# Forgetting attention in a hybrid decoder block: when the weights of the last heads and of the gated unit are fetched

## The chip, the cores and the metric

The kernel runs on one core of a Trainium2 chip. The metric is the device time of one execution in microseconds (us). A core has five engines that each work through their own instructions in order and wait for each other by semaphores: TensorE (PE, matrix products), VectorE (DVE), ScalarE (ACT), GpSimd (POOL) and SyncE (SP). SP does no arithmetic here: it issues most of the DMA transfers, in order, and an issue that has to wait holds up those behind it.

## The reference

Batch 1, sequence 1024, width 1024, all float32. Cut to what matters:

```python
u = rms_norm(h, norm_mix)
u_ssm, q, k, v, f_logit, gate_logits = split(u @ w_in)
y_ssm = gelu(s5_ssm(u_ssm, ...))
glu_a, glu_b = split(y_ssm @ w_glu); out_a = glu_a * sigmoid(glu_b)
att = forgetting_attention(q, k, v, f_logit + b_forget)   # 8 heads of 64, causal softmax, bias from cumsum(log f)
h = h + (gate_a * out_a + gate_b * (att @ w_fox_o)) @ w_mix_out
h = h + memory_cross_attention(...)
h = h + (silu(f_a) * f_b) @ w_ffn_out
return rms_norm(h, norm_final)
```

## The kernel before

A float32 product is made of three products in a reduced format: each operand is split into a high part (`split`, L178: a cast on ACT) and a low part (L179: a subtraction, mostly on DVE), and `mm3` (L168 to L170) adds hi*hi, lo*hi and hi*lo in PSUM. So every weight is loaded into a tile `raw` (a ring of 4), cast on ACT to `whi`, subtracted on DVE to `wlo`, and then used by PE. ACT and DVE work in order, so a cast that waits for its transfer holds up everything behind it there.

The stages are: the input norm and the state-space branch (its output y lies in DRAM as `y_d`), the attention over 8 heads (`Fox.run`, about 300 to 592 us), the tail (gated unit, mixing, cross-attention, feed-forward). The attention is what the change touches. Its loop over heads `h` runs 12 units (two blocks of queries, 4 and 8 blocks of keys); `scores` makes a unit's scores on PE (L1655, L1656, bank `sc`), adds the causal mask on DVE (`trk`, L1658) on the diagonal, takes the exponential on ACT (`pf`, L1662), and splits it into `ph` (ACT L1667, or DVE L1664) and `pl` (DVE L1668 or POOL L1665); `values_hi` and `values_lo` multiply these with v (L1680, L1681, L1687). Between the units stand lists `side[0..11]` of other work for later heads:

- `pro[h + 2].parts` and `.evac`: q and k of the head after the next, 16 products of three matmuls (`uh`, `ul` are the halves of u; names `_0` and `_1` are its two halves of tokens), copied out to the tiles `hb` by L1597 to L1603;
- `row_max(h + 1)` (L1628 on PE, L1630 and L1633 on DVE) and `max_row` (L1642, L1644): the row maxima of the next head, which go by a small DMA (L1645, `hb<-mr`) into the operand of the next head's scores: those scores can't start before it has landed;
- `pro[h + 3].load` (L1575, L1576, two transfers of 256 KB in 256-byte pieces, called in `side[5]`) and `.split` in `side[9]`: the weights of the head three ahead;
- `finish(h - 1)` (L1698 to L1702: `rc<-num`, `rd_d<-rc`, `rb<-rd_d`) and `divide(h - 1)` (L1708, L178, L179, then L1714): the softmax denominator goes through DRAM to be spread over 64 partitions, and the head's result is divided by it;
- in head 6, `load_y` (L1733): y from `y_d` into tiles `yh`, `yl` that take the place of tiles of u, 16 transfers of 256 KB in 512-byte pieces; `gate_rows` (L1610, L1611) for the two gate rows of a later head;
- in head 7, the first products of the gated unit (`Glu.values(0..3)`): `load(j)` (two transfers of `wg_d`, 256 KB each, issued at L153) and `split`, then the products with y.

The order in the text is not the order on the engines: a scheduler moves instructions ahead where their operands allow it. `issue_after(ins)`, here called through `B.behind(ins)`, adds an edge from `ins` to each instruction of the block that is on the engine of `ins`: those are queued behind it there, without a semaphore. All transfers named in this change are issued by SP, so such a block binds only SP's transfers in it, not the casts on ACT or DVE.

Of the kernel before, what the change touches and what calls it, by code (L numbers as in the profile page):

```python
# [19 lines left out]
P = 128  # L20
D = 1024
L = 1024
NT = 8
GRP = 32
NH = 8
# [270 lines left out]
def hybrid_block_kernel(ctx: ExitStack, tc: tile.TileContext, x, mem, norm_mix, w_in, b_forget,  # L296
# [32 lines left out]
    with tc.tile_pool(name="fox", bufs=1, reuse_waits="tile") as fp:  # L329
        Fox(B, fp, sh, uT, w_in, b_forget[0], cum_d, rd_d, att_d).run(y_d, yT, aT, w_glu, wg_d,  # L330
                                                                       [f for j in range(4) for f in glu.values(j)])
    with tc.tile_pool(name="st2", bufs=1, reuse_waits="tile") as s2:
# [170 lines left out]
def stage_tail(B, big, s2, sh, x, glu, aT, gate_d, kv_d, w_fox_o, w_mix_out, g_mq, w_mem_q, w_mem_o, g_ffn,  # L503
# [19 lines left out]
    fox = {}  # L523

    def fox_part(j):
        if j % 2 == 0:
            fox[j // 2] = B.wblock(w_fox_o, 0, 4, j * P, 2 * P)
        fh, fl = fox[j // 2]
        o = (j % 2) * P
        sg = glu.out.pop(j)  # L530
        for h in range(2):
            cs = slice(512 * h, 512 * h + 512)
            po = B.bank("pv")
            B.gemm_t(po, fh[:, :, o:o + P], fl[:, :, o:o + P], aT, h, 4)
            gb = load(gate_d[D + j * P:D + (j + 1) * P, cs], "gb")
            V.tensor_mul(gb, gb, po)
            V.tensor_add(sg[:, cs], sg[:, cs], gb)
            mh, ml = mT.rhs(j, h)
            B.split(mh, ml, sg[:, cs])

    for j in range(8):
        if j > 3:
            for f in glu.values(j):
                f()
        glu.rest(j)
        if j > 2:
            fox_part(j - 3)
# [906 lines left out]
class Fox:  # L1454
# [90 lines left out]
    def setup(self):  # L1545
# [15 lines left out]
        self.pj, self.mc, self.pvs, self.num, self.rb, self.raw = {}, {}, {}, {}, {}, {}  # L1561
        self.hi_todo, self.lo_todo = [], []

# [73 lines left out]
    def max_row(self, h):  # L1637
        B = self.B
        mc = self.mc.pop(h)
        B.V.tensor_tensor(out=mc[:, 0, :], in0=mc[:, 0, :], in1=mc[:, 1, :], op=ALU.max)  # L1640
        pm = B.bank("misc")
        B.T.transpose(pm[0:NT, 0:P], mc[:, 0, :], B.ident)  # L1642
        mr = B.small.tile([NT, P], F32R, tag="mr", bufs=1, name="mr")
        B.V.tensor_scalar(out=mr, in0=pm[0:NT, 0:P], scalar1=-1.0, scalar2=None, op0=ALU.mult)  # L1644
        B.S.dma_start(f32(self.hb[h % 2][2][68:69, :]).rearrange("o (a b) -> o a b", a=NT), f32(mr))  # L1645

# [46 lines left out]
    def finish(self, h):  # L1693
# [7 lines left out]
        rb = self.fp.tile([64, L], F32, tag="rb", bufs=2, name="rb")  # L1701
        self.spread = S.dma_start(rb, self.rd_d[h].partition_broadcast(64))  # L1702
        self.rb[h] = rb
# [17 lines left out]
    def run(self, y_d, yT, aT, w_glu, w_d, filler):  # L1721
# [8 lines left out]
        def load_y(k, h):  # L1730

            for i, dst in enumerate(yT.rhs(k, h)):
                S.dma_start(f32(dst).rearrange("p (t c) -> p t c", t=4),  # L1733
                            y_d[k, i, 4 * h:4 * h + 4].rearrange("t p c -> p t c"))

# [33 lines left out]
        for h in range(NH):  # L1769
# [17 lines left out]
            if h + 3 < NH:  # L1787
                side[9].append(lambda: pro[h + 3].split(self.exp))
            if h > 0 and h + 3 < NH:
                side[5].append(lambda: pro[h + 3].load(self.spread))  # L1790
            if h == 0:
                side[0].append(lambda: self.values_of_v(0, 7))
            if late:
                for k in range(8):
                    side[4 + k].append(lambda k=k: load_y(k // 2, k % 2))
            if h == NH - 1:
                for k in range(3):
                    side[6 + k].append(lambda k=k: load_att(k))
                for i, f in enumerate(filler):
                    side[i * 12 // len(filler)].append(f)  # L1800
            for i, u in enumerate(units):
# [44 lines left out]
```

## Time and profile before

| what | us |
|---|---|
| median of 3 runs (1578.55 to 1581.72) | 1579.52 |
| the profiled execution's own time | 1578.99 |
| its span, first to last instruction | 1577.3 |
| PE busy in the span | 1529.5 |
| DVE busy | 1023.0 |
| ACT busy | 657.7 |

The page of the profile gives busy times per engine, groups of instructions by line with the idle time ahead of them and what ended it, and the chain that ended last. The timeline lists instructions with start, duration, engine, line, output and input, and in brackets the idle time ahead and its releaser. In the view by stretches each row has the stretch, its length, and for PE, PEld (the weight loads), DVE, ACT and POOL the busy time and the number of instructions, then the clock that was granted to TensorE (1.00 is full), the share of time in which the DMA engines were busy, and GB/s.

### The profile page before, as it was taken

The page shows a single profiled execution, that of the slowest core. Times are in us where ns is not written, and L with a number is a line of the kernel's source. Part 1 is how long each engine was busy: PE and PEld are TensorE (multiplying, and loading weights), DVE is VectorE, ACT ScalarE, POOL GpSimd, SP SyncE. Part 2 cuts the span into 40 slices and gives each one's busy share as a digit, 9 for nine tenths or more (in the row PEclk, how much of TensorE's full clock was granted, in tenths as well). Part 3 has the DMA queues.
Part 4 walks back from the last instruction along what each step waited for, and adds up shares of the span by engine and source line. Part 5 has one row for each costly group of instructions (what it writes and reads, how often), then busy time and mean ns, then how long its engine had stood idle before and what let it go on. Part 6 is the DMA issues. An engine that isn't in the chain of part 4 may idle for free.

```text
span 1577.3 us, 20371 instructions
## 1 busy us (share of the span) xinstructions
PE 1529.5 (97%) x7313; PEld 1258.4 (80%) x7313; DVE 1023.0 (65%) x1822; ACT 657.7 (42%) x1177; POOL 264.9 (17%) x343
## 2 busy tenths in 40 slices
PE   7799999999999899999999999999999999999997
PEld 6688888898777578878888788888888888788886
DVE  6756545444788677676455688777777775566555
ACT  6422434323566553232335565333333332354342
POOL 3026653200212124110001200100000000001001
PEclk8999999999999999999999999999999999999999
DMA  8753466332123746368411156554445543896642
GB/s 295 151 106 97 130 116 143 97 119 30 25 45 56 206 121 194 114 206 284 144 28 40 62 206 192 169 164 158 159 155 162 161 148 130 279 391 223 192 155 107
DMA packets 196101, 235.09 MB, mean 149 GB/s; under 512 B 35144, under 2 KB 127208, under 8 KB 195488
## 3 DMA queue, kind: packets, MB, share of 16 engines
q1 hardware_dynamic: 188512, 215.97, 46.6%
q10 hardware_dynamic: 7488, 17.83, 3.0%
q8 instruction: 57, 0.93, 0.2%
q14 instruction: 44, 0.36, 0.1%
HBM read 162.98 MB, written 72.71 MB: 149 GB/s over the span
## 4 chain that ended last, share of the span: by engine, by line
PE 80%; DVE 7%; DMA 5%; ACT 3%; POOL 2%; issue 2%; SPq 0%; POOLq 0%; ACTq 0%; DVEq 0%
PE mm L875 14%; PE mm L168 8%; PE mm L169 8%; PE mm L170 8%; PE pv L875 7%; PE mm L1015 4%; PE sc L875 4%; PE sc L168 3%; PE sc L170 3%; PE sc L169 3%; PE sc L1015 3%; PE pv L1015 3%; PE misc L1015 1%; DMA raw<-in_w_in_dram 1%; DMA raw<-in_w_mem_kv_dram 1%
## 5 line engine op out<-in xcount | busy, mean ns | idle before, releaser
L178 ACT CAST whi<-raw 128x1024 fp32r<-128x1024 f32 (+2 forms) x123 | 114.7, 940 | 176.7 <-PE mm L875 52.8
L179 DVE TENSOR_TENSOR wlo<-raw,whi 128x1024 fp32r<-128x1024 f32 (+2 forms) x120 | 127.7, 1069 | 73.2 <-ACT whi L178 71.3
L168 PE MATMUL mm<-uh,whi 128*128 128x512 f32 x344 | 137.5, 400 | 2.5 <-ACT whi L178 2.4
L179 DVE TENSOR_TENSOR ol<-or,oh 128x1024 fp32r<-128x1024 f32 x73 | 92.1, 1266 | 68.5 <-ACT oh L178 67.5
L170 PE MATMUL mm<-uh,wlo 128*128 128x512 f32 x344 | 135.2, 393 | 0.5 <-DVE wlo L179 0.5
L169 PE MATMUL mm<-ul,whi 128*128 128x512 f32 x344 | 135.4, 394 | 0.0
L178 ACT CAST oh<-or 128x1024 fp32r<-128x1024 f32 x73 | 76.9, 1053 | 104.5 <-PE mm L1015 35.2
L907 POOL TENSOR_TENSOR g<-a,c 128x512 f32<-128x512 f32 x22 | 35.8, 1627 | 386.8 <-ACT a L906 299.0
L1665 POOL TENSOR_TENSOR pl<-pf,ph 128x512 fp32r<-128x512 f32 (+1 forms) x32 | 37.8, 1181 | 242.7 <-DVE ph L1664 173.1
L168 PEld LDWEIGHTS mm<-uh,whi 128*128 128x128 f32 x344 | 65.2, 190 | 14.8 <-ACT whi L178 2.8
L170 PEld LDWEIGHTS mm<-uh,wlo 128*128 128x128 f32 x344 | 64.9, 189 | 14.7 <-DVE wlo L179 1.5
L169 PEld LDWEIGHTS mm<-ul,whi 128*128 128x128 f32 x344 | 65.2, 190 | 11.0
L197 POOL TENSOR_TENSOR r<-ms,mhalf 128x1 f32<-128x1 f32 (+1 forms) x30 | 19.4, 647 | 308.1 <-DVE ms L193 280.8
L1662 ACT ACTIVATE pf<-sc 128x512 f32<-128x512 f32 (+1 forms) x96 | 46.3, 489 | 45.0 <-DVE sc L1658 29.4
L875 PE MATMUL pv<-S3h,we 128*128 128x512 f32 x176 | 57.7, 389 | 0.0
L1131 POOL TENSOR_TENSOR sg<-sg,ga 128x512 f32<-128x512 f32 x16 | 30.5, 1928 | 72.7 <-DVE sg L1124 72.7
L1668 DVE TENSOR_TENSOR pl<-pf,ph 128x512 fp32r<-128x512 f32 (+2 forms) x64 | 35.8, 560 | 10.5 <-ACT ph L1667 9.7
L1015 PE MATMUL mm<-oh 128*128 128x512 f32 x106 | 41.2, 389 | 0.0
L1015 PE MATMUL mm<-ol,oh 128*128 128x512 f32 x106 | 41.2, 389 | 0.0
L1015 PE MATMUL mm<-oh,ol 128*128 128x512 f32 x106 | 41.2, 389 | 0.0
L178 ACT CAST we<-rawb 128x512 fp32r<-128x512 f32 x20 | 12.5, 624 | 68.9 <-PE pv L875 33.8
L168 PE MATMUL sc<-uh,whi 128*128 128x512 f32 x104 | 40.8, 393 | 0.0
(583 smaller groups left out, 4585.0 us busy)
## 6 DMA issues: line engine op xcount, KB each, us to landing
or<-c_d SPq DMA_DIRECT2D x77, 256.0 KB
raw<-in_w_in_dram SPq DMA_DIRECT2D x22, 512.0 KB
wo<-in_w_ffn_out_dram SPq DMA_DIRECT2D x22, 512.0 KB
c_d<-g SPq DMA_DIRECT2D x44, 256.0 KB
t_d<-wo SPq DMA_DIRECT2D x44, 256.0 KB
or<-t_d SPq DMA_DIRECT2D x44, 256.0 KB
rawb<-in_w_ffn_in_dram SPq DMA_DIRECT2D x20, 512.0 KB
raw<-in_w_ffn_in_dram SPq DMA_DIRECT2D x20, 512.0 KB
```

The costliest lines, as they stand in the source:

```text
L168: T.matmul(ps, lh, rh, start=first, stop=False)
L169: T.matmul(ps, lh, rl, start=False, stop=False)
L170: T.matmul(ps, ll, rh, start=False, stop=last)
L178: self.A.copy(hi, src)
L179: (self.G if pool_lo else self.V).tensor_sub(lo, src, f32(hi))
L875: T.matmul(ps, l_[:, k, :], r_, start=first and k == 0 and i == 0, stop=k == 3 and i == 2, skip_group_check=True)
L907: G.tensor_mul(g[:, 512:], a1, c1)
L1015: T.matmul(ps, l_[:, gi], r_[:, 512:], start=n < 3 and p == 0 and k == 0 or n == 7 and p == 0 and k == 0, stop=p == NP - 1 and k == 2, ski ...
L1131: self.B.G.tensor_mul(self.out[j][:, cs], self.out[j][:, cs], ga)
L1662: self.exp = A.activation(pf[:, off:], ps[:, off:], AF.Exp)
L1665: G.tensor_sub(pl[:, off:], pf[:, off:], f32(ph[:, off:]))
L1668: V.tensor_sub(pl[:, off:], pf[:, off:], f32(ph[:, off:]))
```

## The change

Four edits, all of them on the place of transfers in SP's queue:

1. The weights of heads 5, 6 and 7 are loaded one head sooner: heads 4 and 5 in head 1, head 6 in head 2, head 7 in head 3, each behind the spread of the denominators (`rb<-rd_d`) of the head before the one they are called in. The splits stay where they were.
2. `load_y` takes all first halves of the tokens before the second halves; the first halves are queued behind the spread of head 4, the second behind the maxima of head 6 (`hb<-mr`).
3. The loads of the gated unit in head 7's list are queued behind the spread of head 3 (the first three) or behind the maxima of head 6 (the fourth).
4. In the tail, loads of the later gated-unit weights and of `w_fox_o` are queued behind the maxima of head 6.

```diff
-        self.hi_todo, self.lo_todo = [], []
+        self.hi_todo, self.lo_todo, self.spread, self.maxima = [], [], {}, {}
...
-        B.S.dma_start(f32(self.hb[h % 2][2][68:69, :]).rearrange("o (a b) -> o a b", a=NT), f32(mr))
+        self.maxima[h] = B.S.dma_start(f32(self.hb[h % 2][2][68:69, :]).rearrange("o (a b) -> o a b", a=NT), f32(mr))
...
-        self.spread = S.dma_start(rb, self.rd_d[h].partition_broadcast(64))
+        self.spread[h] = S.dma_start(rb, self.rd_d[h].partition_broadcast(64))
...
-            for i, dst in enumerate(yT.rhs(k, h)):
-                S.dma_start(f32(dst).rearrange("p (t c) -> p t c", t=4),
-                            y_d[k, i, 4 * h:4 * h + 4].rearrange("t p c -> p t c"))
+            with B.behind(self.maxima[NH - 2] if h else self.spread[NH - 4]):
+                for i, dst in enumerate(yT.rhs(k, h)):
+                    S.dma_start(f32(dst).rearrange("p (t c) -> p t c", t=4),
+                                y_d[k, i, 4 * h:4 * h + 4].rearrange("t p c -> p t c"))
+
+        def first_glu(i, f):
+            with B.behind(self.spread[3] if i < 9 else self.maxima[NH - 2]):
+                f()
...
-            if h > 0 and h + 3 < NH:
-                side[5].append(lambda: pro[h + 3].load(self.spread))
+            for n_ in {1: (4, 5), 2: (6,), 3: (7,)}.get(h, ()):
+                side[5].append(lambda n_=n_: pro[n_].load(self.spread[h - 1]))
...
-                    side[4 + k].append(lambda k=k: load_y(k // 2, k % 2))
+                    side[4 + k].append(lambda k=k: load_y(k % 4, k // 4))
...
-                    side[i * 12 // len(filler)].append(f)
+                    side[i * 12 // len(filler)].append(lambda i=i, f=f: first_glu(i, f))
...
+    glu.after = fox.maxima[NH - 2]
...
-            fox[j // 2] = B.wblock(w_fox_o, 0, 4, j * P, 2 * P)
+            with B.behind(glu.after):
+                fox[j // 2] = B.wblock(w_fox_o, 0, 4, j * P, 2 * P)
...
-            for f in glu.values(j):
-                f()
+            with B.behind(glu.after):
+                for f in glu.values(j):
+                    f()
```

SP's queue in head 4, before: `raw_4939` is the weights of head 7, `raw_5601`, `raw_5685` and `raw_5770` are the first three of the gated unit, `att_d` is the result of head 3.

```order
L1698 DMA rc_4864<-num_4573 128x1x8
L1700 DMA rd_d_82<-rc_4864 128x8
L1702 DMA rb_4868<-rd_d_82 64x1024
L1575 DMA raw_4939<-in_w_in_dram 128x8x64
L1576 DMA raw_4939<-in_w_in_dram 128x8x64
L153 DMA raw_5601<-wg_d_2919 128x4x128 x2
L1714 DMA att_d_80<-ahi_4914 64x1024
L1714 DMA att_d_80<-alo_4915 64x1024
L153 DMA raw_5685<-wg_d_2919 128x4x128 x2
L153 DMA raw_5770<-wg_d_2919 128x4x128 x2
L1610 DMA hb_3220<-cum_d_81 2x1024
L1645 DMA hb2_3226<-mr_5021 1x8x128
```

The same place in the changed kernel (lines 3 higher).

```order
L1701 DMA rc_4867<-num_4576 128x1x8
L1703 DMA rd_d_82<-rc_4867 128x8
L1705 DMA rb_4871<-rd_d_82 64x1024
L153 DMA raw_5601<-wg_d_2919 128x4x128 x2
L153 DMA raw_5685<-wg_d_2919 128x4x128 x2
L153 DMA raw_5770<-wg_d_2919 128x4x128 x2
L1717 DMA att_d_80<-ahi_4917 64x1024
L1717 DMA att_d_80<-alo_4918 64x1024
L1613 DMA hb_3220<-cum_d_81 2x1024
L1648 DMA hb2_3226<-mr_5021 1x8x128
```

The weights of head 7 have left this place (they stand at the same place of head 3's queue now), and the gated unit's six transfers stand together ahead of head 3's result. On ACT the four casts that belong to these loads stand in the same places as before. In head 1's queue the two transfers of head 5 have been added: the first behind head 4's two, the second behind the result of head 0 and ahead of the gate rows of head 3 and the maxima of head 2.

SP's queue in head 5, before, behind the maxima of head 5: `rc`, `rd_d`, `rb` are head 4's denominators, `yh`, `yl` are y (the number in the middle is the half of the tokens).

```order
L1645 DMA hb2_3226<-mr_5021 1x8x128
L1611 DMA hb_3222<-cum_d_81 2x1024
L1733 DMA yh0_0_2900<-y_d_78 128x4x128
L1698 DMA rc_5146<-num_4858 128x1x8
L1733 DMA yl0_0_2904<-y_d_78 128x4x128
L1733 DMA yh0_1_2901<-y_d_78 128x4x128
L1733 DMA yl0_1_2905<-y_d_78 128x4x128
L1733 DMA yh0_0_2900<-y_d_78 128x4x128
L1733 DMA yl0_0_2904<-y_d_78 128x4x128
L1700 DMA rd_d_82<-rc_5146 128x8
```

The same place in the changed kernel.

```order
L1648 DMA hb2_3226<-mr_5021 1x8x128
L1614 DMA hb_3222<-cum_d_81 2x1024
L1701 DMA rc_5146<-num_4861 128x1x8
L1703 DMA rd_d_82<-rc_5146 128x8
L1705 DMA rb_5150<-rd_d_82 64x1024
L1737 DMA yh0_0_2900<-y_d_78 128x4x128
L1737 DMA yl0_0_2904<-y_d_78 128x4x128
L1737 DMA yh0_0_2900<-y_d_78 128x4x128
L1737 DMA yl0_0_2904<-y_d_78 128x4x128
L1737 DMA yh1_0_2902<-y_d_78 128x4x128
```

No transfer of y is left between the three steps of head 4's denominators; eight of the sixteen follow them, and the other eight come behind the maxima of head 6, seven of them ahead of the gate rows of head 7 and all eight ahead of the gated unit's fourth load.

ACT's order at the start of head 6, before: `whi_5857` is the cast of the gated unit's fourth weights.

```order
L1662 ACTIVATE pf_5334<-sc_5328 128x512
L1689 COPY num_5140<-pv_5232 65x512
L1667 CAST ph_5332<-pf_5334 128x512
L1662 ACTIVATE pf_5359<-sc_5353 128x384
L178 CAST whi_5857<-raw_5854 128x1024
L1667 CAST ph_5357<-pf_5359 128x384
L1662 ACTIVATE pf_5381<-sc_5375 128x256
L1597 ACTIVATE hb2_3226<-mm_5338 64x512
```

The same place in the changed kernel.

```order
L1665 ACTIVATE pf_5334<-sc_5328 128x512
L1670 CAST ph_5332<-pf_5334 128x512
L1665 ACTIVATE pf_5359<-sc_5353 128x384
L1670 CAST ph_5357<-pf_5359 128x384
L1665 ACTIVATE pf_5381<-sc_5375 128x256
L1692 COPY num_5140<-pv_5232 65x512
L1665 ACTIVATE pf_5412<-sc_5406 128x128
L1670 CAST ph_5410<-pf_5412 128x128
```

The cast no longer stands between an exponential and its `ph`; it comes 12 places later, behind `pf_5488`, a unit of the second block of queries. Its subtraction on DVE moves to the end of head 6.

More of the change, by code (lines that the diff above doesn't have):

```diff
@@ L329, in hybrid_block_kernel @@
     with tc.tile_pool(name="fox", bufs=1, reuse_waits="tile") as fp:
-        Fox(B, fp, sh, uT, w_in, b_forget[0], cum_d, rd_d, att_d).run(y_d, yT, aT, w_glu, wg_d,
-                                                                       [f for j in range(4) for f in glu.values(j)])
+        fox = Fox(B, fp, sh, uT, w_in, b_forget[0], cum_d, rd_d, att_d)
+        fox.run(y_d, yT, aT, w_glu, wg_d, [f for j in range(4) for f in glu.values(j)])
+    glu.after = fox.maxima[NH - 2]
     with tc.tile_pool(name="st2", bufs=1, reuse_waits="tile") as s2:
```

## Prediction

> **What bounds the kernel now.** I read the page first, then PE's waits, then the attention in stretches, then the timelines of the engines that PE's longest waits lead to.
>
> ```profile
> PE 1529.5 (97%) x7313; PEld 1258.4 (80%) x7313; DVE 1023.0 (65%) x1822; ACT 657.7 (42%) x1177; POOL 264.9 (17%) x343
> PE 80%; DVE 7%; DMA 5%; ACT 3%; POOL 2%; issue 2%; SPq 0%; POOLq 0%; ACTq 0%; DVEq 0%
> ```
>
> PE is busy for 97% of the span and carries 80% of the chain that ended last. So a change of transfers alone is worth only what PE waits for them, directly or through ACT and DVE. PE's waits from 500 to 580 us (total, times, longest) name the releasers:
>
> ```profile
> PE mm L168 <- ACT whi L178: 2.4, 1, 2.4
> PE pv L1680 <- ACT ph L1667: 2.2, 3, 1.0
> PE sc L1655 <- ACT pf L1662: 2.1, 2, 1.7
> PE mm L170 <- DVE wlo L179: 0.5, 1, 0.5
> PE mm L1628 <- ACT hb L1603: 0.5, 1, 0.5
> ```
>
> Heads 5 and 6 lie here, with 7.7 us of waits. In stretches (busy time of PE, PEld, DVE, ACT, POOL, then granted clock, DMA share, GB/s):
>
> ```profile
> 488.60:512.80 24.20, 24.17 (x119) 18.44 (x118) 19.59 (x51) 15.10 (x30) 4.60 (x4) 1.00 0.27 39
> 512.80:519.70 6.90, 3.39 (x15) 1.78 (x14) 1.88 (x5) 2.78 (x4) 0.00 (x0) 1.00 0.96 266
> 519.70:526.50 6.80, 5.84 (x18) 4.24 (x19) 5.37 (x7) 5.02 (x9) 0.00 (x0) 0.50 0.24 70
> 526.50:539.70 13.20, 13.20 (x67) 10.05 (x65) 10.06 (x30) 7.63 (x16) 3.33 (x3) 1.00 0.95 236
> 539.70:541.80 2.10, 0.41 (x3) 0.05 (x1) 2.10 (x5) 1.64 (x2) 0.00 (x0) 1.00 1.23 291
> 544.30:560.00 15.70, 13.99 (x70) 9.62 (x69) 12.56 (x34) 11.18 (x24) 2.03 (x2) 1.00 0.61 176
> 568.20:592.00 23.80, 23.72 (x115) 17.99 (x114) 16.47 (x29) 10.59 (x23) 5.58 (x5) 1.00 0.43 121
> ```
>
> Head 4 (first row) and head 7 (last row) leave PE no room. Between them lie a stall at 513 to 526 us, in the second half of which TensorE was granted only half its clock, a second one at 540 to 542, and a looser stretch up to 560. ACT's timeline shows what the first one is:
>
> ```profile
> 511.06 0.58 ACT L1603 CAST hb<-mm 64x512 fp32r<-64x512 f32 x1
> 516.17 1.04 ACT L178 CAST whi<-raw 128x1024 fp32r<-128x1024 f32 x1 [4.52 <-DMA raw<-in_w_in_dram]
> 517.23 0.38 ACT L1662 ACTIVATE pf<-sc 128x256 f32<-128x256 f32 x1
> 518.19 1.05 ACT L178 CAST whi<-raw 128x1024 fp32r<-128x1024 f32 x1 [0.58 <-DMA raw<-wg_d]
> 519.15 0.40 ACT L1667 CAST ph<-pf 128x256 fp32r<-128x256 f32 x1
> 520.83 1.04 ACT L178 CAST whi<-raw 128x1024 fp32r<-128x1024 f32 x1 [1.28 <-DMA raw<-wg_d]
> ```
>
> ACT stands at the cast of head 7's weights for 4.52 us and at two casts of the gated unit's for 0.58 and 1.28, because their transfers have not landed; the `pf` and `ph` of head 4's last units stand behind them, and PE behind those. SP's timeline shows why:
>
> ```profile
> 499.55 0.46 SPq L1702 DMA_DIRECT2D rb<-rd_d  x1
> 500.06 0.58 SPq L1575 DMA_DIRECT2D raw<-in_w_in_dram  x1
> 500.69 0.57 SPq L1576 DMA_DIRECT2D raw<-in_w_in_dram  x1
> 501.31 8.29 SPq L153 DMA_DIRECT2D raw<-wg_d  x2
> 509.70 3.05 SPq L1714 DMA_DIRECT2D att_d<-ahi  x1
> 513.44 3.97 SPq L153 DMA_DIRECT2D raw<-wg_d  x4
> ```
>
> Head 7's weights go out at 500, the gated unit's first transfers stall SP for 8.29 us behind them, and the last four leave only at 513.44.
>
> **Part 1, weights a head sooner (with the gated unit's loads in one piece).** Edit 1 and edit 3 act together here. Head 7's weights now leave behind head 3's `rb`, about 25 us (one head, the length of the 488.60 row) ahead of 500; even at the 16 us that they take now, from 500 to the cast at 516.17, they have landed by 491, and their cast comes at 511.64 (511.06 + 0.58). The six transfers of the gated unit stay behind `rb` at 499.55. What six times 256 KB need, from rows of the rate:
>
> ```profile
> 427.50:433.00 5.50, 5.50 (x28) 4.02 (x27) 4.81 (x8) 3.77 (x6) 2.20 (x1) 1.00 0.67 124
> 501.60:509.60 8.00, 8.00 (x39) 5.96 (x38) 7.01 (x15) 5.28 (x9) 1.29 (x1) 1.00 0.40 31
> 516.00:520.30 4.30, 1.94 (x6) 1.19 (x7) 2.34 (x5) 2.78 (x4) 0.00 (x0) 0.93 0.93 280
> ```
>
> The pieces of `raw<-wg_d` (third row) run at 280 GB/s: 1573 KB in 5.6 us, so by about 507. The earliest of their casts can't start before 512.7 (511.64 plus 1.04 for head 7's). All three waits on ACT go: 4.52 + 0.58 + 1.28 = 6.4 us. How much of it reaches the end is bounded by what is late next in 512.8 to 526.5, 13.7 us long: ACT is busy for 2.78 + 5.02 = 7.8 of it, leaving 5.9 to gain; DVE for 1.88 + 5.37 = 7.25, leaving 6.45; PE for 3.39 + 5.84 = 9.2, leaving 4.5, but 5.84 of that at half clock, where a product costs double. I take 6.3, near DVE's row, since DVE must still make four `wlo` in a row ahead of head 5's masks; the ends are 4.5 and 6.45. I add nothing for the clock: at full speed PE would wait here for DVE.
>
> **Part 2, y behind the denominators.** Before, y's loads surround head 4's denominators:
>
> ```profile
> 533.33 0.46 SPq L1702 DMA_DIRECT2D rb<-rd_d  x1
> 538.78 1.22 DVE L1708 TENSOR_TENSOR num<-num,rb 64x1024 f32<-64x1024 f32 x1 [1.77 <-DMA rb<-rd_d]
> 541.75 0.39 PE L1655 MATMUL sc<-hb,hb 69*128 69x256 f32 x1 [1.69 <-ACT pf L1662]
> ```
>
> `rb` needs 5.4 us to land among them; DVE waits 1.77 us at the division, the masks stand behind it, and PE waits 1.69. Now nothing of y is ahead, and DVE waits no more. DVE is late next: it is busy for all 2.10 us of the stretch at 539.70, but that is the work that piled up while it waited. I take 1.7; ends 0.5 and 1.9.
>
> **Part 3, head 6.** The fourth cast of the gated unit leaves its place ahead of a `ph`:
>
> ```profile
> 552.57 1.05 ACT L178 CAST whi<-raw 128x1024 fp32r<-128x1024 f32 x1
> 554.08 0.39 PE L1680 MATMUL pv<-ph,vhi 128*65 128x384 f32 x1 [0.63 <-ACT ph L1667]
> 555.74 0.50 PE L1655 MATMUL sc<-hb 69*128 69x512 f32 x1 [0.40 <-ACT pf L1662]
> 550.88 0.25 SPq L1610 DMA_DIRECT2D hb<-cum_d  x1
> ```
>
> That frees 0.63 + 0.40 = 1.0 us. Against it, seven loads of y now stand ahead of head 7's gate rows (550.88 before) in SP's queue; the last of them must wait until PE has read the last of u, so SP is held there, and the gate rows, and the fourth load of the gated unit behind them, come later, relative to PE, than now. No row shows this; the nearest are the 1.69 above for a row that lands late among loads of y, and 0 if the maxima of head 7 have other work ahead. I take 0.8 of cost, so 0.2 of gain; ends 2.0 lost and 1.0 gained. Edit 4 moves transfers of the tail that are called behind `hb<-mr` anyway: nothing.
>
> **Part 4, the crowd in head 1.** Head 1 now carries 1 MB of weights in place of 512 KB. Behind them in the queue stand the maxima of head 2:
>
> ```profile
> 424.31 0.36 SPq L1700 DMA_DIRECT2D rd_d<-rc  x1
> 425.78 0.52 SPq L1702 DMA_DIRECT2D rb<-rd_d  x1
> 439.95 0.71 SPq L1645 DMA_DIRECT2D hb<-mr  x1
> 443.73 0.40 PE L1655 MATMUL sc<-hb 69*128 69x512 f32 x1
> ```
>
> Now they have 3.8 us from issue to use, and a transfer of their size needs 1.5 when the queue is empty (`rd_d` at 424.31 until `rb`, which waits for it, at 425.78). Head 4's weights are through by 433 (the 427.50 row: 5.5 us at 124 GB/s); the results of head 0, another 512 KB, take 1.9 us at 280 GB/s; 512 KB more at 124 GB/s take 4.2. So the queue empties at about 439 to 440, just as the maxima leave. I take 0.3 of cost; ends 0 and, at half that rate, 4.
>
> [...]
>
> **The sum.** 6.3 + 1.7 + 0.2 - 0.3 = 7.9 us. From the profiled execution's 1578.99 that gives 1571.1; the median of before lies 0.5 higher, so I predict 1571.6. The ends of the four parts added up give 4.5 + 0.5 - 2.0 - 4 = -1 and 6.45 + 1.9 + 1.0 = 9.4; all bad ends at once are not likely.
>
> **The rivals.**
>
> *The wait moves into head 6.* Held at y's second half, SP sends head 7's gate rows and the gated unit's fourth load late, and PE or ACT waits there about 3 us instead of 0.8 (a row's landing of 5.4 us as for `rb`, less the 2 to 3 us of other work ahead). For it: DMA at 0.61 in that stretch before. Against it: the loads now start earlier. Gain 7.9 - 2.2 = 5.7, and 5.0 if the cast on ACT slips by 0.7 as well: 1574.5.
>
> *The half clock is not the stall's doing.* It began at 519.70, behind waits of 2.4 and 0.5 us, and the rows show no other half-clock stretch in the attention; but one case is no proof. If it comes all the same, now over busy PE, 6.8 us at half speed cost up to 3.4, of which I count 3: 1574.6. [...]
>
> *Slower: the crowd in head 1 holds back head 2.* Head 7's weights moved at 31 GB/s for 8 us. If head 5's do so when they stand behind head 4's, 524 KB take 16.9 us; with the 1.9 of head 0's results the queue empties at 433 + 18.8 = 451.8 and the maxima of head 2 land at 453.3. PE waits from 443.73 for 9.6 us, and a half-clock stretch as at 519.70 follows, 3.4. That is 13.0 against 7.9 + 0.3: 4.8 slower, 1584.3. It decides where wait and half clock reach 8.2, so at a wait of 4.8: the queue empty at 447, a rate of 43 GB/s. Against it: the rows of other heads' weights show 124.
>
> *It doesn't do what it says.* If the gated unit's loads, now first behind `rb`, ran at 31 GB/s, they would be as late as now. But in the rows they never did while alone, and even 8 us at 31 followed by 280 ends at 514.5, near their casts. About 1579.
>
> **How the numbers follow.** Chances: forecast 0.67, wait in head 6 0.14, half clock 0.09, no effect 0.05, crowd 0.05. About 0.2%, 3.2 us, is what a measurement of this kernel can tell from no change. The first three cases are faster by more: 0.90. No effect: 0.05 within it. The crowd: 0.05 slower. The range reaches down to the good ends with something for a tighter head 6 (11 us gained), 1568.5, and up past the second and third case, 1575.5; it leaves out the last two.
>
> **What would show each step.** In the changed profile ACT's casts at about 512 to 518 have no DMA wait; the granted clock stays at 1.00 from 513 to 527; SP's six `wg_d` issues take no longer than 6 us in all; the stretch from 512.8 to the end of the half clock at 526.5 is 6 us shorter; DVE's division of head 4 has no wait for `rb`. Wrong would be: a PE wait for `sc` at 444 (crowd), a wait at L1628 or at the fourth cast in head 6, a half-clock stretch without a stall, or stretches from 526 to 568 no shorter than now because DVE is the bound there (it is busy for 80% of 544.30 to 560).

## The result, and the profile after

| | us |
|---|---|
| before, median of 9 runs | 1579.52 (1576.5 to 1581.72) |
| after, median of 9 runs on the same chip | 1572.92 (1570.37 to 1576.72) |
| after / before | 0.9964, 95% interval 0.9954 to 0.9974 |
| profiled execution: span before, after | 1577.3, 1570.4 |
| forecast | 1571.6, range 1568.5 to 1575.5 |

The changed kernel is faster by 0.36%, 5.7 us by the ratio (4.1 to 7.3), 6.6 by the medians; the forecast was 7.9. In the lists of the changed kernel, line numbers of the attention class are 2 to 3 higher than before (L1645 is L1648, L1655 is L1658, L1662 is L1665).

PE's waits from 500 to 580 us (total, times, longest) are 3.7 us where they were 7.7:

```profile
PE sc L1658 <- ACT pf L1665: 1.4, 3, 1.0
PE pv L1683 <- ACT ph L1670: 0.6, 1, 0.6
PE misc L1645 <- DVE mc L1643: 0.6, 1, 0.6
PE pv L1683 <- DVE ph L1667: 0.5, 1, 0.5
PE mm L1631 <- DVE mc L1633: 0.4, 1, 0.4
PE mm L1631 <- ACT hb L1606: 0.2, 1, 0.2
```

The stretch where before had its stall and its half clock (busy PE, PEld, DVE, ACT, POOL, then granted clock, DMA share, GB/s):

```profile
512.80:526.50 13.70, 13.39 (x68) 9.99 (x67) 13.23 (x34) 11.69 (x22) 0.74 (x1) 1.00 0.09 27
```

This gives the size of the gain. In 512.8 to 526.5 PE now does 13.39 us of work at full clock. Before, it did 3.39 us at full and 5.84 at half clock (0.50), which, halved, is 3.39 + 2.92 = 6.31 us of the same work. The difference is 7.1 us, of which 2.9 are the clock and 4.2 the waits. The halving is an estimate from the granted clock: in the timeline of before, products of 128x512 start 0.43 us apart in that stretch and 0.23 at full clock, by which the clock's share would be 2.7.

```profile
505.13 0.39 PE L169 MATMUL mm<-ul,whi 128*128 128x512 f32 x1
505.36 0.39 PE L170 MATMUL mm<-uh,wlo 128*128 128x512 f32 x1
523.68 0.63 PE L169 MATMUL mm<-ul,whi 128*128 128x512 f32 x1
524.11 0.63 PE L170 MATMUL mm<-uh,wlo 128*128 128x512 f32 x1
```

The loads went where the forecast put them. On ACT the casts of head 7's weights and of the gated unit's first three loads have no DMA wait:

```profile
512.72 1.05 ACT L178 CAST whi<-raw 128x1024 fp32r<-128x1024 f32 x1
514.07 1.04 ACT L178 CAST whi<-raw 128x1024 fp32r<-128x1024 f32 x1
515.31 1.05 ACT L178 CAST whi<-raw 128x1024 fp32r<-128x1024 f32 x1
517.71 1.05 ACT L178 CAST whi<-raw 128x1024 fp32r<-128x1024 f32 x1
```

Executions of one program drift against each other outside the attention (the maxima of head 1, ahead of the change, leave at 413.20, 410.94 and 412.97 us in three profiles of the changed kernel), so I follow the change by a clock of its own: the times at which SP issues transfers that both kernels have. Before (the maxima of heads 1, 6 and 7, head 4's denominators, the first transfer behind the attention):

```profile
412.20 0.69 SPq L1645 DMA_DIRECT2D hb<-mr  x1
525.49 0.54 SPq L1698 DMA_DIRECT2D rc<-num  x1
545.32 0.70 SPq L1645 DMA_DIRECT2D hb<-mr  x1
569.30 0.70 SPq L1645 DMA_DIRECT2D hb<-mr  x1
619.13 0.46 SPq L211 DMA_DIRECT2D gbc<-in_norm_mem_q_dram  x1
```

After:

```profile
413.20 0.69 SPq L1648 DMA_DIRECT2D hb<-mr  x1
519.39 0.54 SPq L1701 DMA_DIRECT2D rc<-num  x1
537.59 0.70 SPq L1648 DMA_DIRECT2D hb<-mr  x1
563.91 0.70 SPq L1648 DMA_DIRECT2D hb<-mr  x1
613.44 0.46 SPq L211 DMA_DIRECT2D gbc<-in_norm_mem_q_dram  x1
```

At the maxima of head 1, ahead of the change, this execution runs 1.00 us late. Against that it is 7.1 us early at head 4's denominators (519.39 - 525.49 - 1.00), 8.7 at the maxima of head 6, 6.4 at those of head 7, and 6.7 behind the attention. By these marks head 5 added 1.6 us, and head 6 took back 2.3. The two marks between do not cut PE's work at the same place, though. The stretches from head 4's `rc` to the maxima of head 6 and from there to those of head 7, before (first two rows) and after:

```profile
525.49:545.32 19.83, 18.14 (x88) 13.52 (x88) 15.98 (x42) 11.87 (x22) 4.63 (x4) 0.97 0.94 229
545.32:569.30 23.98, 22.27 (x108) 15.77 (x106) 20.70 (x52) 15.61 (x32) 4.61 (x4) 1.00 0.52 147
519.39:537.59 18.20, 16.94 (x82) 11.81 (x81) 17.72 (x43) 11.77 (x22) 4.60 (x4) 1.00 0.66 160
537.59:563.91 26.32, 23.78 (x114) 16.97 (x112) 18.99 (x51) 16.14 (x32) 4.61 (x4) 1.00 0.71 187
```

Six products that ran ahead of the maxima of head 6 now run behind them. Counted by what PE waits (the length of the stretch less PE's busy time), head 5 gained 0.4 us (1.69 to 1.26) and head 6 lost 0.8 (1.71 to 2.54). Another 0.5 us in head 5 is the end of the half clock, which lasted 1.0 us past head 4's `rc` (525.49 to 526.5). The mark behind the attention has the same number of products ahead of it in every kernel here, so that column of the table below is the one to compare. In head 6 stands a new wait, at the cast of the gated unit's fourth load (ACT's timeline):

```profile
555.07 1.05 ACT L178 CAST whi<-raw 128x1024 fp32r<-128x1024 f32 x1 [2.48 <-DMA raw<-wg_d]
```

On SP the two halves of that load are apart: the second stands behind a store that waits for head 5's reciprocal.

```profile
547.45 0.50 SPq L153 DMA_DIRECT2D raw<-wg_d  x1
549.73 0.34 SPq L1703 DMA_DIRECT2D rd_d<-rc  x1
550.11 0.43 SPq L153 DMA_DIRECT2D raw<-wg_d  x1
```

### The profile page after: what moved, and what is told of

Read it like the earlier page. It is cut to its first block, busy times and chain, and to the rows that moved or that the text cites. A ratio compares the mean times of both kernels' runs of the same rounds, so it can differ in the third digit from the quotient of the medians.

```text
span 1570.4 us, 20364 instructions
## 1 busy us (share of the span) xinstructions
PE 1529.5 (97%) x7313; PEld 1259.6 (80%) x7313; DVE 1024.0 (65%) x1822; ACT 658.6 (42%) x1177; POOL 265.1 (17%) x343
## 4 chain that ended last, share of the span: by engine, by line
PE 81%; DVE 8%; DMA 4%; ACT 3%; POOL 2%; issue 2%; SPq 0%; POOLq 0%; ACTq 0%; DVEq 0%
PE mm L878 14%; PE mm L168 8%; PE mm L170 8%; PE mm L169 8%; PE pv L878 7%; PE mm L1018 5%; PE sc L878 4%; PE sc L1018 4%; PE sc L168 3%; PE sc L170 3%; PE sc L169 3%; PE pv L1018 3%; PE misc L1018 2%; DMA raw<-in_w_in_dram 1%; DMA raw<-in_w_mem_kv_dram 1%
## 5 line engine op out<-in xcount | busy, mean ns | idle before, releaser
L1665 ACT ACTIVATE pf<-sc 128x512 f32<-128x512 f32 (+1 forms) x96 | 46.5, 490 | 44.0 <-DVE sc L1661 28.1
```

The costliest lines, as they stand in the source:

```text
L1665: self.exp = A.activation(pf[:, off:], ps[:, off:], AF.Exp)
```

## The experiments

My theory: the gain is ACT's queue no longer waiting for late weights, with the half clock behind that wait, about 7 us; y's new place gives 1.6; the fourth load takes 2 back in head 6. Rivals: y's order brought the gain; the half clock comes by itself; head 6 is bound by DVE or PE whatever the transfers do; the crowd of transfers costs in head 1. The table puts all runs together. "Shift" is the measure above, in us against before, each counted from the maxima of head 1; it is read from one profile each, the ratio from the timed runs. Two profiles lost 1.4 us in head 1 already (1.5 MB in head 1; the repeat with the tail behind head 5's `rb`).

| kernel | ratio to before (95%) | head 4's `rc` | maxima of 6 | maxima of 7 | behind attention |
|---|---|---|---|---|---|
| changed kernel | 0.9964 (0.9954 to 0.9974) | -7.1 | -8.7 | -6.4 | -6.7 |
| the same, first repeat | 0.9963 (0.9947 to 0.9980) | -7.1 | -8.7 | -6.5 | -6.8 |
| the same, second repeat | 0.9967 (0.9952 to 0.9982) | -7.0 | -8.6 | -7.0 | -7.3 |
| edit 1 undone | 1.0003 (0.9990 to 1.0015) | -0.4 | -1.7 | +2.1 | +1.9 |
| edit 2 undone | 0.9963 (0.9948 to 0.9977) | -7.2 | -7.5 | -7.6 | -7.6 |
| edit 1 alone | 0.9983 (0.9970 to 0.9995) | -3.3 | -2.5 | -2.0 | -2.0 |
| edit 2 alone | 0.9992 (0.9982 to 1.0003) | -0.4 | -1.1 | -0.7 | -1.0 |
| fourth load early | 0.9967 (0.9953 to 0.9980) | -7.1 | -8.7 | -5.7 | -6.0 |
| 1.5 MB in head 1 | 0.9961 (0.9947 to 0.9975) | -5.5 | -7.1 | -1.5 | -1.7 |
| columns exchanged (on before) | 0.9977 (0.9965 to 0.9990) | -4.9 | -3.6 | -3.6 | -3.6 |
| tail behind head 5's `rb` | 0.9968 (0.9953 to 0.9983) | -7.1 | -8.7 | -6.0 | -4.8 |
| the same, repeat | 0.9955 (0.9940 to 0.9970) | -5.8 | -7.5 | -6.8 | -5.6 |
| and all of y's second half | 0.9958 (0.9941 to 0.9975) | -7.1 | -8.7 | -7.4 | -6.5 |

**The changed kernel again**, as the yardstick of two chips.

> The changed kernel once more, unaltered, as the yardstick for the three beside it. From its profile I expect 6.5 us less than before (the median difference was 6.6), with about 1 us either way. In its profile: no DMA wait at ACT's casts of head 4 (before: 4.52, 0.58, 1.28 us), no stretch at half clock behind them, and one wait of about 2.5 us of ACT for the gated unit's fourth load in head 6, behind which DVE's division of head 5 stands about as long.

> The changed kernel unaltered, as the yardstick on this chip for the kernel beside it: 5 to 7 us under before. In its profile, from the maxima of head 1 to the first transfer behind the attention, 6.7 us less than before (6.69 and 6.83 in the two profiles so far): 7.1 gained in head 4, 1.6 in head 5, and 2.0 lost in head 6.

Both came out as the changed kernel had. ACT's wait at the fourth cast is 2.48, 2.35 and 1.49 us in the three profiles, and PE's waits in head 6 follow it: 2.54, 2.40 and 1.57 us in all, where before has 1.71.

**Edit 1 undone.**

```diff
-            for n_ in {1: (4, 5), 2: (6,), 3: (7,)}.get(h, ()):
+            for n_ in {1: (4,), 2: (5,), 3: (6,), 4: (7,)}.get(h, ()):
```

> The changed kernel with edit 1 alone undone: the weights of heads 5, 6 and 7 go out a head later again, the rest stays. My theory: head 7's weights land late again, ACT waits about 4.5 us at their cast and about 2 us at the gated unit's, PE behind it stands 2 to 3 us and then gets half its clock for some 6 us. That loses the 7.1 us which head 4 gained; the 1.6 of the division stays and so do the 2 lost in head 6. So 0 to 1 us less than before, at the level of before. Rival, that the order of y is what brought the time: 4 us or more remain of the gain. Rival, that a waiting engine is not what halves the clock: the waits return and the granted clock stays at 1.00 behind them; then some 3 us of the 7 do not return, and the time is 3 us under before.

The whole gain is gone. ACT's wait and the half clock are back at the same place; the first row is ACT's, the others are stretches:

```profile
515.66 1.04 ACT L178 CAST whi<-raw 128x1024 fp32r<-128x1024 f32 x1 [4.49 <-DMA raw<-in_w_in_dram]
```

```profile
512.80:519.70 6.90, 3.71 (x17) 2.22 (x16) 2.54 (x5) 2.78 (x4) 0.00 (x0) 0.97 0.96 270
519.70:526.50 6.80, 5.49 (x18) 3.95 (x17) 4.92 (x8) 5.33 (x10) 0.00 (x0) 0.52 0.08 19
```

The rival that y's order brought the time falls. The profile lost more than I expected: head 6 costs 3.8 us here (-1.7 to +2.1), of which 1.7 are a stretch at half clock from 563.6 to 567.2. So edits 2 to 4 without edit 1 are worth nothing.

**Edit 2 undone, and edit 2 alone.** The first is the changed kernel with y's loads as before, the second is before with y's loads as now.

```diff
-            with B.behind(self.maxima[NH - 2] if h else self.spread[NH - 4]):
-                for i, dst in enumerate(yT.rhs(k, h)):
+            for i, dst in enumerate(yT.rhs(k, h)):
...
-                    side[4 + k].append(lambda k=k: load_y(k % 4, k // 4))
+                    side[4 + k].append(lambda k=k: load_y(k // 2, k % 2))
```

> The changed kernel with edit 2 alone undone: y's sixteen loads surround head 4's denominators again. My theory: the stall of head 4 stays away (7.1 us gained), the division of head 4 waits for rb again by about 1.7 us, and head 6 runs as before, without the 2.5 us wait at the fourth cast, since y's second half no longer stands ahead of it. So 5.5 to 7 us less than before, within 1 us of the changed kernel: edit 2 gave in head 5 what it took in head 6. Rival, that head 6 lost its 2 us to DVE, which is simply busy there once the stall ahead is gone: then head 6 is as slow here too, and the time is 1.5 to 2 us over the changed kernel's.

> Before with edit 2 alone: y's loads behind named transfers, all else as before. My theory: the stall of head 4 stays with its half clock; head 4's division no longer waits for rb. So 1 to 2 us less than before. Rival, that the crowd of transfers in heads 4 to 6 as a whole made the stall: 4 us or more.

Without edit 2 the division of head 4 waits for `rb` again (DVE), and head 6 has no wait at the fourth cast (ACT):

```profile
532.46 1.22 DVE L1711 TENSOR_TENSOR num<-num,rb 64x1024 f32<-64x1024 f32 x1 [1.57 <-DMA rb<-rd_d]
```

```profile
546.24 1.05 ACT L178 CAST whi<-raw 128x1024 fp32r<-128x1024 f32 x1
```

Its shift stays at -7.5 all through head 6, so my rival, that a busy DVE makes head 6 slow as soon as the stall ahead is gone, fails for y's old order. Its time is that of the changed kernel. Alone, edit 2 gives 0.9992, which can't be told from nothing. So no gain of edit 2 shows in the time: by the marks it gains 1.3 us up to the maxima of head 6, and they are gone by those of head 7.

**Edit 1 alone.** The diff is that of edits 2 to 4 taken back; the lines on the weights stay.

> Before with edit 1 alone: the weights of heads 5, 6 and 7 a head sooner; the gated unit's and y's loads are called as before, which lets the first three loads of the gated unit go out by themselves behind head 7's weights in heads 3 and 4. My theory: this alone removes the stall of head 4, 7.1 us in all; head 4's division waits for rb as before, head 6 runs as before. So 5.5 to 7 us less than before, the same as the changed kernel within 1 us. Rival, that the gated unit's loads in one piece are needed for the gain of head 4: one to two of ACT's waits stay, and 2 to 4 us less than before.

My expectation missed, and the rival has the size by another way. 2.7 us are gained, and the waits of head 4 are gone; the loss is at places that neither named, above all head 3. Without a named transfer ahead of them the gated unit's loads leave directly behind head 7's weights (SP):

```profile
477.06 0.57 SPq L1577 DMA_DIRECT2D raw<-in_w_in_dram  x1
477.67 9.30 SPq L153 DMA_DIRECT2D raw<-wg_d  x2
...
492.65 0.71 SPq L1646 DMA_DIRECT2D hb<-mr  x1
```

SP is held for 9.30 us, the maxima of head 4 leave 2.1 us late, and PE waits for them; a stretch at half clock follows (PE's timeline, then stretches):

```profile
496.85 0.68 PE L1656 MATMUL sc<-hb 69*128 69x512 f32 x1 [2.19 <-DMA hb<-mr]
```

```profile
496.00:498.00 2.00, 1.15 (x3) 0.97 (x4) 0.01 (x1) 0.00 (x0) 0.00 (x0) 0.75 0.77 229
498.00:500.00 2.00, 2.00 (x8) 1.72 (x8) 0.79 (x3) 1.67 (x4) 0.00 (x0) 0.50 0.00 0
```

In head 5, with y's loads as before, PE waits 2.19 us once more, at 539.84, and 3.4 us at half clock follow. So edit 1 needs edit 3 beside it: the stall of before has moved a head ahead with the slow weights, and the kernel with edit 2 undone, which has edits 1, 3 and 4, has no such wait. Edits 3 and 4 were not taken back one by one. The row also shows the half clock behind a stall at another time and for another reason (2.19 us for `hb<-mr` at 496.85, then 0.50 from 498 to 500), against the rival by which it comes by itself.

**Why head 7's weights are slow.** Before, with nothing else than the columns of two heads exchanged. Heads 4 and 7 then work with each other's q and k, so it computes something else than the reference, with the same work:

```diff
-            src = lambda c: self.w_in[:, c + h * DH:c + (h + 1) * DH].rearrange("(k p) c -> p k c", p=P)
+            n = {4: 7, 7: 4}.get(h, h)
+            src = lambda c: self.w_in[:, c + n * DH:c + (n + 1) * DH].rearrange("(k p) c -> p k c", p=P)
```

> Before with the columns of the weights of heads 4 and 7 exchanged, and nothing else: head 4 computes with head 7's and head 7 with head 4's. In both traces the 256-byte pieces of head 7's weights ran at about 110 pieces per us where those of heads 4 to 6 ran at 240 to 500, whatever stood beside them. If the columns are slow: what is fetched in head 4 (now head 4's columns) lands in 5 to 8 us instead of 15, the waits of ACT at 512 to 521 us shrink to under 2 us together, and with them goes the half-clock stretch; the load in head 1 takes 14 to 15 us instead and is late for its cast there, or just in time. Then 3 to 7 us less than before if head 1 hides it, about before's time if the stall moves to head 1, and there a half-clock stretch would follow it as in head 4. Rival, the place is slow (the gated unit's loads beside it, the time of the run): the waits in head 4 stay as they are and so does the time, within 0.7 us.

It is the columns. Fetched in head 1, they move at 27 GB/s in the stretch where head 4's own moved at 124, and ACT waits there; the stall of head 4 is gone, and the half clock with it:

```profile
427.50:433.00 5.50, 5.50 (x26) 3.84 (x25) 5.30 (x9) 3.84 (x6) 2.21 (x1) 1.00 0.40 27
512.80:519.70 6.90, 6.90 (x38) 5.34 (x37) 6.82 (x14) 6.39 (x12) 0.00 (x0) 1.00 0.55 158
519.70:526.50 6.80, 6.48 (x33) 4.55 (x32) 6.30 (x21) 5.15 (x11) 0.76 (x2) 1.00 0.72 198
```

```profile
439.09 1.04 ACT L178 CAST whi<-raw 128x1024 fp32r<-128x1024 f32 x1 [3.14 <-DMA raw<-in_w_in_dram]
```

PE's waits behind that cast are 1.02 and 0.53 us and no half clock follows (1.00 from 438 to 450). By the marks head 4 gains 7.1 us here, as much as in the changed kernel, and the slow load has cost 2.2 by the maxima of head 4. By the ratio the exchange gives 3.6 us (1.6 to 5.5) against 5.7 for the whole change. Not all of the load is slow. In the changed kernel, where it stands in head 3, the first 8 us and the next 2 show:

```profile
478.00:486.00 8.00, 8.00 (x40) 5.89 (x39) 7.19 (x14) 5.27 (x10) 1.28 (x1) 1.00 0.45 36
486.00:488.00 2.00, 2.00 (x11) 1.40 (x10) 1.97 (x5) 1.95 (x5) 1.28 (x1) 1.00 0.77 110
```

At 36 GB/s about 290 KB move in the 8 us, little more than the first of the load's two transfers (q's columns, 256 KB); the rest goes at 110. That it is q's columns alone no run separates, and why they are slow the runs don't tell.

**1.5 MB in head 1.**

```diff
-            for n_ in {1: (4, 5), 2: (6,), 3: (7,)}.get(h, ()):
+            for n_ in {1: (4, 5, 6), 2: (7,)}.get(h, ()):
```

> The changed kernel with head 6's weights fetched in head 1 too and head 7's in head 2: 1.5 MB of weights in head 1 instead of 1 MB (0.5 MB before), all ahead of the maxima of head 2 on SP's queue. The forecast had a rival, the crowd, by which these maxima come late from 43 GB/s down; the changed kernel showed no such wait. My theory: with 512 KB more ahead of them the maxima land 2 to 5 us late, PE waits at the first scores of head 2 (about 444 us) by that much, so 1 to 5 us over the changed kernel. Rival, that the queue has room for it: no wait there and the time of the changed kernel within 0.7 us.

The rival held: the maxima of head 2 leave at 440.50, PE has no wait for them, and the time is that of the changed kernel. The 1.4 us lost in head 1 in this profile are a wait for DVE at 432, and the profile of another kernel below, with the changed kernel's loads in head 1, has the same. The crowd is no danger here. Its profile shows what the wait of head 6 can become. PE's wait (first fence) and the stretch behind it:

```profile
557.82 0.69 PE L1658 MATMUL sc<-hb 69*128 69x384 f32 x1 [2.32 <-ACT pf L1665]
```

```profile
558.00:560.00 2.00, 2.00 (x6) 1.35 (x7) 1.55 (x3) 0.41 (x1) 0.00 (x0) 0.50 0.19 53
```

**Head 6: the waits taken away one by one.** First the fourth load whole and early: `fetch` issues the two transfers of a load, which the cast later takes over, and a step of head 5 calls it for all four.

```diff
+            if h == 5:
+                for j in range(4):
+                    side[5].append(lambda j=j: fetch_glu(j))
...
+        def fetch_glu(j):
+            with B.behind(self.spread[3] if j < 3 else self.spread[4]):
+                fetch(j)
```

> The changed kernel with one thing different: all four loads of the gated unit are issued by a step of head 5, the first three behind head 3's rb as now, the fourth, both halves, directly behind head 4's rb and ahead of y, in place of behind the maxima of head 6. The casts stay where they are. My theory: the fourth load lands some 20 us ahead of its cast, the 2.48 us wait of ACT in head 6 and the 2.48 us wait of DVE at the division behind it are gone, and the time is 1.5 to 2 us under the changed kernel's, 8 to 8.5 under before. Rival, DVE or head 7's gate rows bound head 6: the wait of ACT goes and the time stays within 0.5 us of the changed kernel's. Second rival: 512 KB more ahead of y delay y's first half, which nobody needs before the tail; nothing from that.

The cast no longer waits, and the time is the same. The wait moved to DVE, which now stands at head 5's division for `rb`, and PE behind it by way of ACT (DVE's timeline, PE's timeline):

```profile
561.62 1.22 DVE L1720 TENSOR_TENSOR num<-num,rb 64x1024 f32<-64x1024 f32 x1 [2.23 <-DMA rb<-rd_d]
```

```profile
564.46 0.39 PE L1667 MATMUL sc<-hb 69*128 69x256 f32 x1 [1.92 <-ACT pf L1674]
```

Then everything of the tail and the last four loads of y behind that `rb`, in two runs of one kernel; in a last kernel `late_y` is `self.spread[NH - 3]` for every k, so that all of y's second half is behind it:

```diff
-    glu.after = fox.maxima[NH - 2]
+    glu.after = fox.spread[NH - 3]
...
-            with B.behind(self.maxima[NH - 2] if h else self.spread[NH - 4]):
+            late_y = self.maxima[NH - 2] if k < 2 else self.spread[NH - 3]
+            with B.behind(late_y if h else self.spread[NH - 4]):
```

> The kernel with the gated unit's fourth load behind head 4's rb, and one thing more: the last four loads of y, the output projection's weights and the tail's gated weights leave behind head 5's rb in place of behind the maxima of head 6. My theory: head 6 lost its time to transfers that stand ahead of rb. With the fourth load early the wait only moved, to DVE's division of head 5, which waited 2.23 us for rb, issued behind y's last loads and 512 KB of the projection's weights. Now only eight loads that are mostly through stand ahead of it: rb lands in about 3 us instead of 8, DVE does not wait for it, PE's wait of 1.92 us in head 6 shrinks under 0.7, and the attention is 8 to 8.7 us shorter than before's, 1.3 to 2 shorter than the changed kernel's. Head 7's maxima must still land in time behind 2.5 MB more (8.7 us at 290 GB/s from about 554, so by 563 for a use at about 569). Rival, DVE or PE's own work bounds head 6: both waits go and the time from head 6's maxima to head 7's stays within 0.5 us of the 26.2 us of the changed kernel. Rival, the crowd moves on: head 7's maxima land late and PE waits for them by 2 us or more.

> The kernel with everything of the tail behind head 5's rb once more, for a second profile of the same program: in the first one head 6 had no DMA wait left, but 6.8 us at half clock from 551 on, behind PE waits of 0.73 and 0.56 only, and the attention was 4.8 us shorter than before's, not 8 to 8.7. If that stretch was chance: none this time, and the attention is 8 us or more shorter, with a timed median like the changed kernel's. Rival, that this order brings it on: the stretch is there again at 550 to 558 and the attention is 4 to 6 us shorter.

> The same with all of y's second half behind head 5's rb, so that nothing but head 5's own denominators moves on the queues between the maxima of head 6 and that rb. If transfers beside rc and rb still held head 6: the wait from rc to rd_d and to rb shrinks by up to 1 us, and the attention is 0.5 to 1 us shorter than in the kernel beside it. If DVE and ACT bound head 6: the stretch from head 6's maxima to head 7's takes as long as beside it, 25.3 to 26.7 us unless the clock is halved in it. Head 7's maxima stand behind 2 MB here, some 7 us at 290 GB/s, and should still be in time. By the timed median no kernel of this series has been told apart from the changed kernel, and I expect the same here, within 1.5 us.

No DMA wait is left on DVE and ACT in head 6, and PE's longest wait is 0.7 us (second profile, 536 to 572 us):

```profile
PE sc L1667 <- ACT pf L1674: 1.0, 2, 0.7
```

Yet none of the three runs is faster than the changed kernel beyond the intervals, and no profile reaches the 8 us that I expected. The first lost 3.4 us to a stretch at half clock (shown at the end) and the last kernel 1.7, from 550.6 to 554.0. But the repeat, without one, comes to 5.6, and to 6.9 if it is counted from head 2, behind the 1.4 us that this profile lost in head 1. My theory of head 6 falls: the fourth load was the last wait there, not the bound. What stands next is DVE. The repeat where PE waits and behind it, and the changed kernel over heads 4 and 5 (stretches):

```profile
548.00:551.00 3.00, 1.71 (x10) 0.93 (x7) 2.87 (x7) 1.84 (x4) 0.00 (x0) 1.00 0.03 1
551.00:557.60 6.60, 6.12 (x27) 4.30 (x28) 6.57 (x15) 4.23 (x7) 2.58 (x2) 1.00 1.04 247
557.60:564.00 6.40, 6.40 (x33) 4.62 (x31) 6.34 (x14) 3.19 (x8) 1.30 (x1) 1.00 0.69 165
```

```profile
505.00:540.00 35.00, 33.57 (x160) 23.93 (x158) 33.76 (x75) 25.73 (x46) 7.17 (x6) 1.00 0.53 132
```

With hardly a transfer moving (1 GB/s), DVE is busy for 2.87 of 3.00 us and PE for 1.71, and DVE stays full up to 564. In the 8 us ahead of 548 it is not (5.01 us). In the changed kernel DVE is busy for 33.76 of the 35 us from 505 on, around and behind the removed stall. So what is saved on transfers there meets a full DVE. That DVE is the bound of the later part of head 6 rests on these rows; no kernel here took work from DVE, so it is not shown by a run of its own.

## Why the prediction was right, and where not

The sum was 7.9 us, the profile gives 6.7 (6.8 and 7.3 in the repeats), the ratio 5.7. The range and the sign held, and part 1 had the right mechanism. But its term was too small by 0.8 to 1.3 us, and parts 2 and 3 together were too large by over 2, so that the sum came near is in part luck. Two of the signs that the forecast had named against itself came true: the wait at the fourth cast, and the heads behind the half clock no shorter than before (from head 4's `rc` to the mark behind the attention 93.64 us before, 94.05 after).

- **Part 1, 6.3 forecast, 7.1 measured at head 4's `rc`, and 0.5 behind it.** Edits 1 and 3 removed all three waits of ACT, and undoing edit 1 brings back the stall and the whole time. The step that failed is "I add nothing for the clock": by the count over 512.8 to 526.5, 2.9 of the 7.1 us are the half clock; products of 128x512 started 0.43 us apart there against 0.23, 1.9 times as far where the forecast has double. The bounds from the busy shares of ACT and DVE (5.9 and 6.45) were too low, as part of what DVE had to do there could be done later: from the maxima of head 4 to head 4's `rc` it is busy for 24.2 us where it was for 25.6. The way that would have given the size is PE's work at full clock, 13.39 against 6.31. That the two edits act together was right: edit 1 alone gives 2.7 by the ratio.
- **Part 2, 1.7 forecast, 0.4 measured by PE's waits, nothing at the end.** DVE's wait for `rb` went as forecast, from 1.77 us to none. But the 1.6 us that the marks show in head 5 come near 1.7 by luck: 0.5 are the half clock's end, and most of the rest is products that moved behind the mark. The failed step is the sentence that DVE's busy share was only "the work that piled up while it waited": DVE is full from 505 to 540 in the changed kernel, and in place of one wait of 1.69 us PE has several smaller ones there, 1.26 in all.
- **Part 3, +0.2 forecast, -0.8 measured by PE's waits** (-0.7 in one repeat, +0.1 in the other), -2.3 by the marks. The failed step is the 0.8 of cost. The two waits that were to go, 0.63 and 0.40, are gone, but 2.5 us stand in their place: 1.0 behind the fourth cast, which waits 2.48 us where it stands now (none behind the 1.49 us of one repeat), and 1.5 in four short waits for ACT and DVE that the forecast did not name. The rival that the wait moves into head 6 had the place and the queue right, the fourth load behind a held SP, and its 5.7 is just what the ratio gives, nearer than the forecast. But without those waits (three kernels) the time is the same, so this term and that of part 2 are one: what head 5 wins is not kept.
- **Part 4, -0.3 forecast, 0.0 measured.** The shifts at the maxima of heads 2 to 4 are within 0.15 us in its three profiles, and 50% more weights there made no wait for them either.
- **In head 4 the half clock is the stall's doing**: three kernels have it with the stall there (granted clock from 519.7 to 526.5: 0.50 before, 0.52 with edit 1 undone, 0.53 with edit 2 alone), and without the stall it is absent there in every profile of the others (1.00 from 512.8 to 526.5 in the changed kernel). The rival that it comes in this place anyway is refuted. In other places PE waits of 2.19 us (edit 1 alone, at 496.85) and 2.32 us (1.5 MB in head 1, at 557.82) came with a stretch at 0.50 too.

## What to carry to other kernels

Before moving transfers, ask which one is slow, by its own rate: here about half of one head's weights ran at a quarter of the rate of head 4's (31 GB/s before, against 124), and what was queued behind them on SP came late with them (its next issue was held for 8.29 us). Price a stall by the work that PE would have done in it at full clock, the half clock behind it included (13.39 against 6.31 us here). And when a wait is gone, look at the busy share of the engine that is next over the whole stretch, not only at the few us around the wait: behind a full DVE (33.76 of 35.00 us) a second and a third removed wait were worth nothing here. A mark in one engine's queue is a clock only as long as the same work stands ahead of it: count the products between two marks before their shift is called a gain.

## What the runs showed of the hardware that was not expected

- Some columns of a weight matrix are fetched at a quarter of the rate of head 4's, with the same shape and piece size, in three places of the program: 27 (head 1, columns exchanged), 36 (head 3, changed kernel) and 31 GB/s (head 4, before) against 124 (head 1, before) in the stretches shown.
- The half clock came in two sizes. From 300 us to 10 us before the end, the profiles of these kernels show stretches that cost 3.4 or 1.7 us of clock each, that is 6.8 or 3.4 us at 0.50: 3.4 before (519.7 to 526.5), with edit 2 alone (520 to 528), with 1.5 MB in head 1 (556 to 564) and with the tail behind head 5's `rb` (550 to 558), 1.7 with edit 1 alone (496 to 502), with the columns exchanged (534 to 540) and with all of y's second half behind `rb` (550 to 554). In the attention all six PE waits from 2.19 us up came with one (2.42 before, at 517.26, and its like with edit 1 undone and with edit 2 alone; the two of 2.19 with edit 1 alone; 2.32 with 1.5 MB in head 1). Of two of 1.92 (fourth load early, at 564.46) and 2.04 (columns exchanged, at 533 to 536) only the longer did, and 1.69 before, at 541.75, had none. But shorter waits had one at times. The kernel with the tail behind head 5's `rb` had one behind waits of 0.73 and 0.56 us, in a stretch where PE was busy for 1.70 of 3.00 us, the kernel after it a shorter one behind waits of 0.72 and 0.56, and the repeat, with 0.74 and 0.56, none:

```profile
548.00:551.00 3.00, 1.70 (x10) 0.93 (x8) 2.87 (x7) 1.85 (x4) 0.00 (x0) 1.00 0.05 7
551.00:557.60 6.60, 6.55 (x17) 4.53 (x18) 6.14 (x14) 3.91 (x7) 2.55 (x2) 0.51 0.87 256
```

At about 373 us, ahead of all that the change touches, PE has the same two waits of 0.8 and 0.6 us in all 14 profiles. Six of them show 3.4 us at half clock behind these waits, eight none (edit 1 undone, then the first repeat of the changed kernel):

```profile
372.80:376.00 3.20, 3.17 (x8) 2.51 (x9) 1.96 (x5) 0.00 (x0) 0.00 (x0) 0.50 0.02 6
372.80:376.00 3.20, 3.07 (x13) 2.23 (x14) 2.51 (x9) 0.00 (x0) 0.00 (x0) 1.00 0.07 13
```

So the same work gets such a stretch in one execution and not in the next, at a cost of 1.7 or 3.4 us. What decides between them stays open. By my estimate it makes a part of the spread of some 6 us between executions of one kernel (1570.37 to 1576.72 for the changed one), which is also why differences under 2 us could not be told apart here.
